# A hybrid attention block on one Trainium2 core: PSUM shared out as two banks for the projections' products and three for scores, instead of three and two

## The chip, the cores and the metric

The kernel runs on one core of a Trainium2 chip. The metric is device time in microseconds (us). TensorE multiplies matrices and writes its sums to PSUM, a memory of eight banks of 2 KB in each of 128 partitions. VectorE (DVE), ScalarE (ACT) and GpSimd (POOL) do elementwise work; SyncE (SP) issues the DMAs between the core's SBUF and the chip's memory. Each engine has its own instruction queue and runs it in order. An instruction whose operand or whose output buffer is not ready stops everything behind it on its engine, and on no other.

## The reference, cut to what matters

One block of a model for 2048 tokens of width 1024, in float32:

```python
# ada: six vectors (scale, shift, gate for the mixer and the FFN) from the condition c
h = rmsnorm(x, g_mix) * (1 + scale) + shift
p = h @ w_in                        # 1024 -> 2 x 256 (gating), 3 x 384 (stick), 3 x 384 (dilated)
a = gelu(u) * (causal 128x128 mixing of rmsnorm(gelu(v)) + b_sp)        # spatial gating, 4 groups

# stick-breaking attention, 6 heads of 64, every key before the query:
z = q @ k.T / 8
weight = sigmoid(z) * prod over the keys between of sigmoid(-z)
o_b = weight @ v

# dilated window attention, 6 heads, 129 keys at distances 0, d, ... 128 d with d = 1, 4, 16:
z = q @ k_gathered.T / 8;  pr = softmax(z);  o_c = pr @ v_gathered     # q and k rotated (rope)
o_c *= softmax over the three d of the log of each softmax's denominator

x = x + gate * (concat(a, o_b, o_c) @ w_out)
x = x + gate2 * convffn(rmsnorm(x))       # up to 2 x 2816, causal convolution of 3 taps, gate, down
out = rmsnorm(x) * g_final
```

## The kernel before, in words

**Products.** Each float32 operand is split into a high and a low part, and a product is three matmuls (high x high, low x high, high x low; L100 to L102). An input projection of a 128-wide block of features for 512 tokens thus takes 8 x 3 = 24 matmuls of 512 columns into one PSUM bank, the tile `gm`; one for values takes 48 matmuls of 256 columns into the tile `gmv`, which has the tag `gm` too. When the last of them is done, ScalarE or VectorE copies the bank to SBUF: as tile `stage`, for queries and keys (then stored to the chip's memory in `bq`, `bk` or, rotated, `cq`, `ck`), or as `vst`, for values. That copy is called the eviction below.

**Stages.** The tokens are worked in two halves of 1024, c = 0 and c = 1. Up to 97 us lie the conditioning vectors, the norm of the first tokens and the first projections. Then come projections, the six stick heads of the first half, the gating of the first half, and the projections of the second half, one stick head of the first half (at about 520 to 580 us) and the six dilated heads of all tokens (460 to 776 us) beside them. From 776 us the second half's stick heads run beside the output projection. The conv-FFN takes from about 1320 us to the end.

**A stick head** (`stick`) loads keys (`khat`, L83) and queries (`q`). For each block of 128 queries and up to 512 keys it has two score matmuls into a bank `z` (L534, L537, and L536 where the causal border lies in the block), two sigmoids on ScalarE (L539 to SBUF as `beta`, L540 back into the bank), a scan along the keys on VectorE (L545, `excl`), which is the last reader of the bank and frees it, a multiply on GpSimd (L78), transposes back on TensorE into a bank `tr` (L554), two copies of that as high and low part (`wh`, `wl`), and the product with the values into the bank `av` (L565). **A dilated head** (`dilated`) has the same shape: scores into a bank `zc` of tag `z` (L620, L621), mask and maximum on VectorE (L623, last reader of the bank), the exponential on ScalarE (L632, `ec`), transposes `trc` (L635), product `avc` (L658). After each 512 queries `fold` (L487) adds the two halves of `av` or `avc` into the one buffer `ys`, which is stored (`yT`, `yc`) before the next sum may be written.

**What sets the order.** Buffers come from pools with a count for each tag (the table `BUFS`): a tile waits until the last reader of the tile that had its slot before is done. In PSUM up to the end of the first half's attentions and all dilated heads there is the pool `ps`: eight banks, as `gm` 3, `z` 2, `tr` 2, `av` 1. At the token `rel` of the string `ORDER` it is given back and the pool `ps2` taken, with `gm` 2 and `z` 3 (L1102). The order in which each engine's queue is filled is chosen when the program is built, by a scheduler that takes ready instructions by their place in the program and by durations that it assumes; the counts of the pools thus change the queues of all engines. On TensorE matmuls of a projection and of an attention stand mixed, so that the one fills the time in which the other waits. The first four query and key products of all (L910, L925) are filled in parts as the conditioning vectors come, in banks named one by one.

Of the kernel before, what the change touches and what calls it, by code (L numbers as in the profile page):

```python
# [5 lines left out]
F32 = mybir.dt.float32  # L6
# [6 lines left out]
PSUM = bass.MemoryType.PSUM  # L13
DRAM = bass.MemoryType.DRAM

P = 128
# [5 lines left out]
TG = 512  # L22
# [21 lines left out]
class Kernel:  # L44
# [810 lines left out]
    def run(self):  # L855
        tc, nc, i = self.tc, self.nc, self.i
        self.constants()
        self.ps = _Bufs(self.pool("ps", space=PSUM), BUFS)
        self.p1 = _Bufs(self.pool("p1"), BUFS)
        self.pa = _Bufs(self.pool("pa", side="right"), BUFS)  # L860
        dr = self.dr
# [27 lines left out]
        def h_cols(c, tg, xs, ks=range(KB)):  # L889

            if hT[c][0][tg] is None:
                hT[c][0][tg], hT[c][1][tg] = self.act_tiles(self.p1, "h", tg)
            self.norm_cols(self.p1, self.ps, "tr", xs, self.cols["a1"], self.cols["s1"], hT[c][0][tg], hT[c][1][tg], ks,
                           ("lnt0", "hlo0") if c == 0 and tg == 0 else ("lnt", "hlo"))
# [5 lines left out]
        def qk_cols(p):  # L900
# [6 lines left out]
        near = (self.p1, "whi"), (self.p1, "wlo")  # L907
        places = ((near, near), (near, ((self.pa, "khat"), (self.pa, "khat"))),
                  (((self.pa, "vhat"), (self.pa, "khat")), ((self.pa, "vhat"), (self.pa, "wl"))))
        banks = [self.ps.tile([P, TG], F32, name="gm", tag=tag) for tag in ("gm", "gm", "gm", "z")]  # L910
        vbanks = [self.ps.tile([P, 2, 256], F32, name="gmv", tag=tag) for tag in ("z", "av")]
        for q in range(4):
            self.ada_first(q)
# [110 lines left out]
        def work(units, what, n, c):  # L1024

            b_qk, c_qk, v, a = units
            if what == "bqk":
                return b_qk(n)
            if what == "cqk":
                return c_qk(n, cs)  # L1030
            if what == "v":
                return v(n)
            if what == "a":
                return a()
            if what == "wout":
                return self.out_weights(ada[2])
            if what == "op":
                return self.out_proj(0)
            return self.out_proj(1, EARLY)

        def finish(names=None):

            while aside and (names is None or any(x[0] in names for x in aside)):
                for _ in aside.pop(0)[1]:
                    pass

        for c, order in enumerate(ORDER):
            u = units(c, hT[c])
            for token in order.split():
                name = token.lstrip("~")  # L1050
# [18 lines left out]
                elif what in ("bqk", "cqk", "v", "a", "wout", "op", "oa"):  # L1069
                    for _ in work(u, what, n, c):  # L1070
                        pass
                    if behind:
                        behind.__exit__(None, None, None)
                        behind = None
                elif what == "vh":
                    finish()
                    if xs is None:
                        xs = h_rows(1, 0)
                    xs2 = []

                    def middle():
                        h_cols(1, 0, xs)
                        xs2.append(h_rows(1, 1))
                    for _ in u[2](n, {1: middle, 3: lambda: h_cols(1, 1, xs2[0])}):
                        pass
                elif what == "hr":
                    xs = h_rows(1, 0)
                elif what == "rope":
                    cs = self.rope_tables(c)
                elif what == "ada":  # L1090
                    with tc.issue_after(self.stored.ins):
                        ada[n] = self.ada_rest(n)
                elif what == "dil":
                    finish([f"cqk{n // 2}{c}", f"v{(6 + n) // 4}{c}"])
                    self.dilated(n)
                elif what == "scales":
                    self.dilated_scales()
                elif what == "rel":
                    finish()
                    self.p1.release()  # L1100
                    self.ps.release()
                    self.ps = _Bufs(self.pool("ps2", space=PSUM), {**BUFS, "gm": 2, "z": 3})  # L1102
                    self.po = _Bufs(self.pool("po"), BUFS)
                elif what == "free":
                    finish()
                    self.pa.release()
                    self.pw = _Bufs(self.pool("pw", side="right"), BUFS)
                    self.pn = _Bufs(self.pool("pn", side="right"), BUFS)
# [43 lines left out]

ENGINES = {"whi0": "a", "wlo0": "v", "lnt0": "a", "hlo0": "v", "lnt": "va", "lnx00": "avv", "lnx01": "aav", "lnx10": "v", "lnx11": "v", "lnx": "va", "hlo": "v", "whi": "a", "wlo": "v", "qkhi": "avv", "qklo": "v", "cqk": "a", "rot1": "v", "rot2": "v", "rot3": "v", "rothi": "aav", "rotlo": "v", "sgu1": "v", "sgu2": "v", "sguhi": "a", "sgulo": "v", "ya": "aaav", "fold": "a", "beta": "p", "whi_s": "a", "whi_d": "avv", "wom": "v", "wohi": "aav", "wolo": "v", "ysc": "v", "yhi": "av", "ylo": "v", "wuhi": "v", "wulo": "pvv", "wdm": "p", "wdhi": "av", "wdlo": "ppv", "upc": "av", "gv": "pppv", "ghi": "ap", "glo": "ppv", "vhi": "av", "vlo": "v", "uc": "v"}

BUFS = {"gm": 3, "z": 2, "tr": 2, "av": 1, "wraw": 2, "whi": 3, "wlo": 3, "s8": 3, "cs": 2, "tmp2": 2, "khat": 3, "vhat": 2, "q": 2, "beta": 4, "excl": 3, "wh": 2, "wl": 2, "fold": 1, "ys": 1, "stat": 2, "mx": 2, "x4": 2, "yraw": 2, "ysc": 4, "yh": 2, "yl": 2, "xo": 3, "wuraw": 4, "wul": 3, "wuh": 3, "wdraw": 2, "fx": 2, "up": 3, "dn": 5, "wdh": 2, "wdl": 2, "upc": 3, "cv": 3, "gh": 4, "gl": 4, "fs": 4, "fry": 2, "frr": 2}

WOUT = 6
EARLY = (0, 1, 5, 6, 7)
# [39 lines left out]
```

## Time and profile before

| | |
|---|---|
| median of 3 runs | 2775.93 us (2775.42 to 2779.58) |
| the profiled execution | 2772.08 us |
| its span, first to last instruction | 2770.4 us |
| mean granted TensorE clock | 0.981 |
| TensorE busy | 2626.6 us, 95%, 13430 matmuls |
| VectorE busy | 2109.4 us, 76% |
| ScalarE busy | 1025.6 us, 37% |
| GpSimd busy | 857.5 us, 31% |
| chain that ended last, by engine | PE 65%, DVE 14%, DMA 10%, ACT 6%, issue 3% |

The program on the chip takes the span and about 1.7 us around it. TensorE's matmuls overlap their neighbours in the records (one of 512 columns is recorded as 0.39 us long and follows the one before by less), so a busy share near 100% does not say that nothing is lost; gaps and the clock tell more. The shares are means over stages: the FFN, from 1320 us on, is more than half of the span and has no tile of this pool.

### The profile page before, as it was taken

What the parts mean: (1) busy time and instruction counts of PE and PEld (TensorE: products, weight loads), DVE (VectorE), ACT (ScalarE), POOL (GpSimd) and SP (SyncE); (2) the same over time, 40 slices, a digit from 0 to 9 for tenths busy, and PEclk for the clock granted to TensorE, in tenths of its full rate; (3) what the DMA queues carried; (4) which work ended last, traced back from release to release, by engine and by line L of the source; (5) the groups of instructions that cost most, each with busy time, mean ns of one, the idle gap of its engine ahead of it and who ended that gap; (6) DMA issues with size and microseconds to landing.
All of it is one profiled execution on the core that took longest, in us unless ns stands there. A gap on an engine that the chain in (4) does not pass through costs nothing.

```text
span 2770.4 us, 36801 instructions
## 1 busy us (share of the span) xinstructions
PE 2626.6 (95%) x13430; PEld 2201.3 (79%) x13430; DVE 2109.4 (76%) x3227; ACT 1025.6 (37%) x1918; POOL 857.5 (31%) x878
## 2 busy tenths in 40 slices
PE   6989999899878999999999999999999999999998
PEld 5878998889857777877788888888877888888886
DVE  5487877666689988756877778777888778777877
ACT  5355554444556666534121212111462111121114
POOL 0032101110045444303334443433433433433423
PEclk9999999999999999999999999999999999999999
DMA  7645586789563333286111111111233111111111
GB/s 238 195 131 171 186 266 190 204 211 233 135 186 101 109 111 86 61 275 219 46 46 46 54 51 49 48 52 46 77 103 107 49 47 54 46 46 46 46 38 61
DMA packets 305296, 309.37 MB, mean 112 GB/s; under 512 B 65516, under 2 KB 245596, under 8 KB 305116
## 3 DMA queue, kind: packets, MB, share of 16 engines
q1 hardware_dynamic: 305116, 307.02, 37.6%
q8 instruction: 107, 1.75, 0.3%
q14 instruction: 73, 0.60, 0.1%
HBM read 232.36 MB, written 68.30 MB: 109 GB/s over the span
## 4 chain that ended last, share of the span: by engine, by line
PE 65%; DVE 14%; DMA 10%; ACT 6%; issue 3%; SPq 1%; POOL 0%; DVEq 0%; ACTq 0%; POOLq 0%
PE up L94 11%; PE up L93 11%; PE up L92 11%; PE dn L94 5%; PE dn L92 5%; PE dn L93 5%; DVE excl L545 3%; DMA wraw<-in_w_in_dram 2%; PE gmv L342 2%; DMA wada<-in_w_ada_dram 2%; PE av L565 2%; DVE wl L78 1%; PE gm L100 1%; PE tr L554 1%; PE gm L101 1%
## 5 line engine op out<-in xcount | busy, mean ns | idle before, releaser
L92 PE MATMUL up<-gh,wuh 128*128 128x512 f32 x1408 | 553.4, 393 | 2.1 <-ACT gh L260 2.1
L94 PE MATMUL up<-gh,wul 128*128 128x512 f32 x1408 | 554.9, 394 | 0.0
L93 PE MATMUL up<-gl,wuh 128*128 128x512 f32 x1408 | 554.5, 394 | 0.0
L78 POOL TENSOR_TENSOR beta<-beta,excl 128x127 f32<-128x127 f32 (+2 forms) x240 | 267.5, 1116 | 869.6 <-DVE excl L545 758.5
L829 DVE TENSOR_TENSOR acc<-dn,acc 128x512 f32<-128x512 f32 x688 | 440.7, 680 | 104.2 <-PE dn L94 102.0
L787 DVE SCALAR_TENSOR_TENSOR cv<-upc,cw,cv 128x512 f32<-128x512 f32 x352 | 334.8, 952 | 104.9 <-ACT cv L785 101.6
L92 PEld LDWEIGHTS up<-gh,wuh 128*128 128x128 f32 x1408 | 265.0, 188 | 62.1 <-ACT gh L260 2.3
L93 PEld LDWEIGHTS up<-gl,wuh 128*128 128x128 f32 x1408 | 265.1, 188 | 61.3 <-issue 0.2
L94 PEld LDWEIGHTS up<-gh,wul 128*128 128x128 f32 x1408 | 265.1, 188 | 60.0 <-issue 0.2
L92 PE MATMUL dn<-wdh,gh 128*128 128x512 f32 x688 | 270.9, 395 | 10.6 <-DVE acc L829 9.4
L93 PE MATMUL dn<-wdl,gh 128*128 128x512 f32 x688 | 270.9, 394 | 0.0
L94 PE MATMUL dn<-wdh,gl 128*128 128x512 f32 x688 | 256.1, 395 | 0.0
L785 ACT ACTIVATE cv<-up,cb 128x512 f32<-128x512 f32 x176 | 136.4, 775 | 290.9 <-DVE upc L72 290.9
L545 DVE TENSOR_TENSOR_SCAN excl<-z,excl,beta 128x512 f32<-128x512 f32 x144 | 183.3, 1275 | 14.9 <-ACT z L540 13.2
L70 ACT ACTIVATE upc<-up 128x512 f32<-128x512 f32 x88 | 52.4, 596 | 373.8 <-PE up L94 373.8
L70 ACT ACTIVATE wh<-tr 128x128 fp32r<-128x128 f32 (+2 forms) x240 | 127.7, 535 | 168.4 <-PE tr L554 164.8
L72 DVE CAST wuh<-wuraw 128x512 fp32r<-128x512 f32 x176 | 129.0, 771 | 62.0 <-PE up L93 59.7
L342 PE MATMUL gmv<-whi,hh 128*128 128x256 f32 x576 | 167.0, 291 | 0.7 <-DVE vst L78 0.7
L342 PE MATMUL gmv<-wlo,hh 128*128 128x256 f32 x576 | 166.6, 290 | 0.3 <-DVE wlo L78 0.3
L342 PE MATMUL gmv<-whi,hl 128*128 128x256 f32 x576 | 166.7, 291 | 0.0
L78 DVE TENSOR_TENSOR wl<-tr,wh 128x128 fp32r<-128x128 f32 (+2 forms) x240 | 141.9, 594 | 31.6 <-ACT wh L70 31.6
L92 PEld LDWEIGHTS dn<-wdh,gh 128*128 128x128 f32 x688 | 129.8, 189 | 42.6 <-DVE acc L829 11.6
(238 smaller groups left out, 5594.8 us busy)
## 6 DMA issues: line engine op xcount, KB each, us to landing
wuraw<-in_w_up_dram SPq DMA_DIRECT2D x176, 256.0 KB, 3.2
wdraw<-in_w_down_dram SPq DMA_DIRECT2D x44, 512.0 KB, 3.5
wada<-in_w_ada_dram SPq DMA_DIRECT2D x32, 512.0 KB, 6.2
wraw<-in_w_in_dram SPq DMA_DIRECT2D x112, 128.0 KB, 4.3
vd<-vst SPq DMA_DIRECT2D x12, 1024.0 KB, 6.0
q<-bq SPq DMA_DIRECT2D x48, 256.0 KB, 4.2
q<-cq SPq DMA_DIRECT2D x48, 256.0 KB, 5.5
x<-xo SPq DMA_DIRECT2D x24, 512.0 KB, 5.2
```

Of the source, the lines that this page charges most:

```text
L70: self.nc.scalar.activation(out, in_, AF.Copy)
L72: self.nc.vector.tensor_copy(out, in_)
L78: (self.nc.vector if eng == "v" else self.nc.gpsimd).tensor_tensor(out=out, in0=a, in1=b, op=op)
L92: self.nc.tensor.matmul(ps, ah, bh, start=(k == 0), stop=False)
L93: self.nc.tensor.matmul(ps, ah, bl, start=False, stop=False)
L94: self.nc.tensor.matmul(ps, al, bh, start=False, stop=(k == n - 1))
L342: self.nc.tensor.matmul(ps[:, e, :], a[:, o:o + P], b, start=(n == 0), stop=(n == 3 * KB - 1))
L545: nc.vector.tensor_tensor_scan(x[:, x0:x0 + n][:, ::-1], z[:, :n][:, ::-1], b[:, :n][:, ::-1], before, op0=ALU.mult, op1=ALU.bypass)
L565: last = nc.tensor.matmul(av[:, q0:256], vhat[kc // 2][:, (kc % 2) * 4 + e, :], w[:, e, q0:256], start=(kc == top and m == 0), stop=(kc == ...
L785: nc.scalar.activation(t, ps, AF.Identity, bias=self.cb[:, blk:blk + 1], scale=self.cw[2][:, blk:blk + 1])
L787: nc.vector.scalar_tensor_tensor(out=t, in0=u[:, tap:tap + TG], scalar=self.cw[tap][:, blk:blk + 1], in1=t, op0=ALU.mult, op1=ALU.add)
L829: nc.vector.tensor_tensor(out=acc[t][:, ns], in0=ps, in1=acc[t][:, ns], op=ALU.add)
```

## The change

The pool `ps` gets two banks for `gm` and three for `z`; `tr` and `av` stay. The pool `ps2` takes the table as it is, which now has the counts that were written out for it, so that nothing changes there. The third of the first four products goes into a bank of tag `z` instead of `gm`.

```diff
-        banks = [self.ps.tile([P, TG], F32, name="gm", tag=tag) for tag in ("gm", "gm", "gm", "z")]
+        banks = [self.ps.tile([P, TG], F32, name="gm", tag=tag) for tag in ("gm", "gm", "z", "z")]
         vbanks = [self.ps.tile([P, 2, 256], F32, name="gmv", tag=tag) for tag in ("z", "av")]
...
-                    self.ps = _Bufs(self.pool("ps2", space=PSUM), {**BUFS, "gm": 2, "z": 3})
+                    self.ps = _Bufs(self.pool("ps2", space=PSUM), BUFS)
...
-BUFS = {"gm": 3, "z": 2, "tr": 2, "av": 1, "wraw": 2, "whi": 3, "wlo": 3, "s8": 3, ...
+BUFS = {"gm": 2, "z": 3, "tr": 2, "av": 1, "wraw": 2, "whi": 3, "wlo": 3, "s8": 3, ...
```

No instruction is added or taken away, but the scheduler fills the queues in another order. On every engine the orders are alike up to the first stick head, and again nearly alike from the second half's first stick head (`z_8433`) on. Three places follow; the number behind a name counts the tiles of the program, and is the same in both.

The first is on TensorE, at the first stick head (about 113 to 121 us). Before, its first two scores, `z_1127` and `z_1141`, stand behind all 24 matmuls of the projection tile `gm_2217` and 6 of the next, `gm_2243`:

```order
L100 MATMUL gm_2243<-hh_716,whi_2192 128x512
L101 MATMUL gm_2243<-hl_724,whi_2192 128x512
L102 MATMUL gm_2243<-hh_716,wlo_2193 128x512
L534 MATMUL z_1127<-khat_1117,q_1121 128x128
L536 MATMUL z_1127<-after_678,ident_r_676 128x128
L537 MATMUL z_1127<-khat_1117,q_1121 128x128
L534 MATMUL z_1141<-khat_1117,q_1121 128x256
L536 MATMUL z_1141<-after_678,ident_r_676 128x128
```

Now three scores of this head stand behind the first 8 of the 24 matmuls of `gm_2217`:

```order
L100 MATMUL gm_2217<-hh_233,whi_2192 128x512
L101 MATMUL gm_2217<-hl_241,whi_2192 128x512
L534 MATMUL z_1127<-khat_1117,q_1121 128x128
L536 MATMUL z_1127<-after_678,ident_r_676 128x128
L537 MATMUL z_1127<-khat_1117,q_1121 128x128
L534 MATMUL z_1141<-khat_1117,q_1121 128x256
L536 MATMUL z_1141<-after_678,ident_r_676 128x128
L537 MATMUL z_1141<-khat_1117,q_1121 128x256
L534 MATMUL z_1162<-khat_1117,q_1121 128x384
L536 MATMUL z_1162<-after_678,ident_r_676 128x128
L537 MATMUL z_1162<-khat_1117,q_1121 128x384
L102 MATMUL gm_2217<-hh_233,wlo_2193 128x512
```

They have moved ahead by 22 matmuls of 512 columns. On SyncE the load of their keys (`khat_1117`) stands ahead of the two stores of `bq10` from `stage_996`, and behind them before; ahead of that both queues have the same DMAs there.

The second is ScalarE and TensorE where the first half's rotation tables are made (about 150 to 160 us). `gm_2284` and `gm_2310` are two projection tiles whose evictions ScalarE does one after the other into `stage_2283`. Before, ScalarE has them here, behind the transposed weights `tr_1272`; the cosine and the sine stand 9 and 8 rows ahead of the first of them, ahead of the sigmoids of `z_1305`:

```order
L70 ACTIVATE wh_1247<-tr_1257 128x4x128
L539 ACTIVATE beta_1335<-z_1332 128x512
L540 ACTIVATE z_1332<-z_1332 128x512
L70 ACTIVATE wh_1247<-tr_1272 128x4x128
L70 ACTIVATE stage_2283<-gm_2284 128x512
L70 ACTIVATE stage_2283<-gm_2310 128x512
L539 ACTIVATE beta_1350<-z_1347 128x512
L540 ACTIVATE z_1347<-z_1347 128x512
L70 ACTIVATE rot_2275<-rot_2275 128x1024
```

Now the sigmoids of `z_1305` and `z_1332` stand ahead of the cosine, and those of `z_1347` and `z_1401`, with the copy of `tr_1299`, between the sine and the evictions:

```order
L381 ACT_TABLE_LOAD
L381 ACTIVATE cos_1378<-cos_1378,halfpi_1089 128x1024
L382 ACTIVATE sin_1377<-sin_1377,sign_1084 128x1024
L70 ACTIVATE wh_1247<-tr_1272 128x4x128
L539 ACT_TABLE_LOAD
L539 ACTIVATE beta_1350<-z_1347 128x512
L540 ACTIVATE z_1347<-z_1347 128x512
L70 ACTIVATE wh_1287<-tr_1299 128x3x128
L539 ACTIVATE beta_1405<-z_1401 128x128
L540 ACTIVATE z_1401<-z_1401 128x128
L70 ACTIVATE stage_2283<-gm_2284 128x512
L70 ACTIVATE stage_2283<-gm_2310 128x512
```

On TensorE the tile `gm_2375`, which now takes the bank of `gm_2284`, has its 24 matmuls right behind the last of `gm_2310` before:

```order
L101 MATMUL gm_2310<-hl_730,whi_2204 128x512
L102 MATMUL gm_2310<-hh_722,wlo_2205 128x512
L100 MATMUL gm_2375<-hh_231,whi_2350 128x512
L101 MATMUL gm_2375<-hl_239,whi_2350 128x512
L102 MATMUL gm_2375<-hh_231,wlo_2351 128x512
```

Now 42 rows of the stick heads stand between the two, and then `gm_2375`:

```order
L565 MATMUL av_1211<-wh_1247,vhat_1119 128x256
L565 MATMUL av_1211<-wl_1248,vhat_1119 128x256
L565 MATMUL av_1211<-wh_1247,vhat_1119 128x256
L565 MATMUL av_1211<-wl_1248,vhat_1119 128x256 x2
L554 MATMUL tr_1315<-ident_60,beta_1309 128x128 x4
L100 MATMUL gm_2375<-hh_231,whi_2350 128x512
L101 MATMUL gm_2375<-hl_239,whi_2350 128x512
L102 MATMUL gm_2375<-hh_231,wlo_2351 128x512
```

The evictions have moved behind the sigmoids of two more score tiles and one more copy, and the start of `gm_2375` behind work of the stick heads alone.

The third is ScalarE near the end of the dilated heads (about 700 to 720 us). Before, the split of a weight tile, `whi_8207`, and a gelu (`u_7827`) stand ahead of the exponentials of the last head, `ec_7046` and `ec_7069`:

```order
L70 ACTIVATE whi_7889<-wraw_7895 128x512
L70 ACTIVATE fold_6962<-avc_6928 64x512
L70 ACTIVATE whc_7012<-trc_7005 128x512
L70 ACTIVATE whi_8207<-wraw_8209 128x512
L425 ACT_TABLE_LOAD
L425 ACTIVATE u_7827<-u_7827 128x1024
L632 ACT_TABLE_LOAD
L632 ACTIVATE ec_7046,stat_7040<-ec_7046,mx_7041 128x128 x2
L632 ACTIVATE ec_7069,stat_7040<-ec_7069,mx_7041 128x128 x2
```

Now the exponentials of this head begin ahead of the splits of `whi_7889`, and the gelu and `whi_8207` stand 6 and 8 rows behind the second of these:

```order
L632 ACTIVATE ec_7046,stat_7040<-ec_7046,mx_7041 128x128 x2
L632 ACTIVATE ec_7069,stat_7040<-ec_7069,mx_7041 128x128 x2
L70 ACTIVATE fold_7023<-avc_6989 64x512
L632 ACTIVATE ec_7099,stat_7040<-ec_7099,mx_7041 128x128 x2
L632 ACTIVATE ec_7122,stat_7040<-ec_7122,mx_7041 128x128 x2
L70 ACTIVATE fold_7091<-avc_7063 64x512
L632 ACTIVATE ec_7152,stat_7040<-ec_7152,mx_7041 128x128 x2
L70 ACTIVATE whc_7112<-trc_7107 128x2x128
L632 ACTIVATE ec_7175,stat_7040<-ec_7175,mx_7041 128x128 x2
L70 ACTIVATE whi_7889<-wraw_7891 128x512
L70 ACTIVATE whi_7889<-wraw_7895 128x512
```

`ec_7046` and `ec_7069` have moved from behind `whi_8207` to 18 and 17 rows ahead of it. TensorE's queue has the last head's `avc` tiles closer together than before: the first matmuls of the last four (`avc_7063`, `avc_7116`, `avc_7169`, `avc_7222`) stand 46, 50 and 41 rows apart, and 54, 48 and 73 before.

## Rows read from the trace of the kernel before

**Rows 1.** Windows: stretch, length, busy us of each engine, PEclk, DMA share, GB/s.
```profile
460.00:520.00 60.00, 53.19 (x356) 49.31 (x355) 44.24 (x86) 18.64 (x49) 0.00 (x0) 0.91 0.97 261
...
580.00:700.00 120.00, 115.29 (x845) 107.52 (x844) 75.68 (x249) 53.60 (x157) 0.00 (x0) 1.00 0.91 231
700.00:776.00 76.00, 67.56 (x469) 63.19 (x468) 45.58 (x129) 35.95 (x76) 0.00 (x0) 0.93 0.56 131
```

**Rows 2.** Waits of TensorE, 60 to 170 us: us in total, times, longest.
```profile
PE z L534 <- DVE excl L545: 5.0, 3, 3.6
```

**Rows 3.** Waits of TensorE, 170 to 520 us.
```profile
PE z L534 <- DVE excl L545: 5.5, 7, 3.1
```

**Rows 4.** Waits of TensorE, 520 to 600 us.
```profile
PE z L534 <- DVE excl L545: 4.5, 1, 4.5
```

**Rows 5.** Waits of TensorE, 700 to 770 us.
```profile
PE trc L635 <- ACT ec L632: 8.4, 2, 7.5
```

**Rows 6.** Waits of TensorE, 45 to 770 us, the whole stretch of the change.
```profile
PE trc L635 <- ACT ec L632: 14.1, 8, 7.5
...
PE zc L620 <- DMA khat<-ck: 3.5, 1, 3.5
PE zc L620 <- DVE stat L623: 3.0, 3, 1.3
```

**Rows 7.** Windows right after four of these waits.
```profile
157.00:164.00 7.00, 5.95 (x15) 4.75 (x16) 7.00 (x7) 4.59 (x9) 4.34 (x3) 0.51 0.47 108
243.00:246.00 3.00, 3.00 (x14) 3.00 (x15) 3.00 (x4) 0.87 (x2) 2.12 (x2) 0.52 0.00 0
536.00:539.00 3.00, 3.00 (x8) 2.32 (x8) 2.08 (x5) 1.36 (x5) 1.83 (x3) 0.50 0.92 263
714.00:724.00 10.00, 5.06 (x25) 5.07 (x26) 4.24 (x15) 7.61 (x17) 0.00 (x0) 0.51 0.85 187
```

**Rows 8.** Timeline of TensorE: start, duration, line, operation, [idle before it].
```profile
118.70 0.39 PE L102 MATMUL gm<-hh,wlo 128*128 128x512 f32 x1
118.93 0.39 PE L100 MATMUL gm<-hh,whi 128*128 128x512 f32 x1
...
120.33 0.33 PE L534 MATMUL z<-khat,q 128*128 128x128 f32 x1 [0.55 <-DMA khat<-bk]
```

**Rows 9.** Timeline of TensorE at 158 us.
```profile
158.05 0.80 PE L534 MATMUL z<-khat,q 128*128 128x512 f32 x1 [3.62 <-DVE excl L545]
```

**Rows 10.** Timeline of TensorE in the dilated attention.
```profile
707.03 0.28 PE L342 MATMUL gmv<-wlo,hh 128*128 128x256 f32 x1
707.15 0.28 PE L342 MATMUL gmv<-whi,hl 128*128 128x256 f32 x1
```

**Rows 11.** Timeline of SyncE's DMA queue.
```profile
112.27 1.24 SPq L83 DMA_DIRECT2D bq<-stage  x2
...
114.38 0.75 SPq L83 DMA_DIRECT2D khat<-bk  x1
```

**Rows 12.** Timeline of ScalarE at 150 to 160 us.
```profile
154.30 1.28 ACT L539 ACT_TABLE_LOAD   x1
...
158.55 1.10 ACT L70 ACTIVATE stage<-gm 128x512 f32<-128x512 f32 x2
```

**Rows 13.** Timeline of TensorE, the last matmul of `gmv_5267`.
```profile
488.65 0.28 PE L342 MATMUL gmv<-whi,hl 128*128 128x256 f32 x1
```

**Rows 14.** Timeline of ScalarE, the evictions of `gmv_5267` and the next.
```profile
504.73 0.64 ACT L70 ACTIVATE vst<-gmv 128x256 fp32r<-128x256 f32 x2
```

**Rows 15.** Timeline of ScalarE at the end of the dilated heads.
```profile
714.08 0.63 ACT L70 ACTIVATE whi<-wraw 128x512 fp32r<-128x512 f32 x1 [8.13 <-DMA wraw<-in_w_in_dram]
...
718.39 0.40 ACT L632 ACTIVATE ec<-ec,mx 128x128 f32<-128x128 f32 x1
```

**Rows 16.** The chain that ended last, 600 to 730 us: start, us, what.
```profile
637.05 7.37 DMA yc<-ys
```

**Rows 17.** DMA issues: KB each, median us from issue to landing.
```profile
yc<-ys SPq DMA_DIRECT2D x24, 128.0 KB, 5.5
```

More of the change, by code (lines that the diff above doesn't have):

```diff
@@ L1153 @@
 ENGINES = {"whi0": "a", "wlo0": "v", "lnt0": "a", "hlo0": "v", "lnt": "va", "lnx00": "avv", "lnx01": "aav", "lnx10": "v", "lnx11": "v", "lnx": "va", "hlo": "v", "whi": "a", "wlo": "v", "qkhi": "avv", "qklo": "v", "cqk": "a", "rot1": "v", "rot2": "v", "rot3": "v", "rothi": "aav", "rotlo": "v", "sgu1": "v", "sgu2": "v", "sguhi": "a", "sgulo": "v", "ya": "aaav", "fold": "a", "beta": "p", "whi_s": "a", "whi_d": "avv", "wom": "v", "wohi": "aav", "wolo": "v", "ysc": "v", "yhi": "av", "ylo": "v", "wuhi": "v", "wulo": "pvv", "wdm": "p", "wdhi": "av", "wdlo": "ppv", "upc": "av", "gv": "pppv", "ghi": "ap", "glo": "ppv", "vhi": "av", "vlo": "v", "uc": "v"}
-BUFS = {"gm": 3, "z": 2, "tr": 2, "av": 1, "wraw": 2, "whi": 3, "wlo": 3, "s8": 3, "cs": 2, "tmp2": 2, "khat": 3, "vhat": 2, "q": 2, "beta": 4, "excl": 3, "wh": 2, "wl": 2, "fold": 1, "ys": 1, "stat": 2, "mx": 2, "x4": 2, "yraw": 2, "ysc": 4, "yh": 2, "yl": 2, "xo": 3, "wuraw": 4, "wul": 3, "wuh": 3, "wdraw": 2, "fx": 2, "up": 3, "dn": 5, "wdh": 2, "wdl": 2, "upc": 3, "cv": 3, "gh": 4, "gl": 4, "fs": 4, "fry": 2, "frr": 2}
+BUFS = {"gm": 2, "z": 3, "tr": 2, "av": 1, "wraw": 2, "whi": 3, "wlo": 3, "s8": 3, "cs": 2, "tmp2": 2, "khat": 3, "vhat": 2, "q": 2, "beta": 4, "excl": 3, "wh": 2, "wl": 2, "fold": 1, "ys": 1, "stat": 2, "mx": 2, "x4": 2, "yraw": 2, "ysc": 4, "yh": 2, "yl": 2, "xo": 3, "wuraw": 4, "wul": 3, "wuh": 3, "wdraw": 2, "fx": 2, "up": 3, "dn": 5, "wdh": 2, "wdl": 2, "upc": 3, "cv": 3, "gh": 4, "gl": 4, "fs": 4, "fry": 2, "frr": 2}
 WOUT = 6
```

## The prediction, made before the changed kernel ran

> **What bounds the kernel now.** TensorE is busy for 95% of the span, so the first question is where its 5% are, and whether the change reaches them. It can reach only the tiles of the first PSUM pool, up to 776 us. I went first through the windows by stage: in the stretch of the first dilated heads, 460 to 520 us, TensorE is busy for 53.19 of 60 us at a mean clock of 0.91, and in the last one, 700 to 776 us, for 67.56 of 76 us at 0.93; between 580 and 700 us it is nearly full, with DMA at 0.91 of its capacity [rows 1]. Then the waits of TensorE say which buffer or value it stood for. The scores of the stick heads waited for a z bank, freed by the scan on VectorE: 5.0 us up to 170 us, 5.5 us from there to 520 us and 4.5 us once at 535 us [rows 2 to 4]. The dilated heads waited 14.1 us for exponentials, 3.0 us for a bank freed by the maximum, and 3.5 us for keys on their way [rows 6]. Next to nothing was lost to a projection that stood for its gm bank. So the third gm bank is spare where the second z bank is short, and that is the argument for a gain.
>
> The windows behind the long waits show a second price: after a wait of some 3 us TensorE's clock is granted at its lower level, 1.2 instead of 2.4 GHz: 0.51, 0.52, 0.50 and 0.51 in four stretches of 7, 3, 3 and 10 us [rows 7]. The time lost there is length times one minus the clock: 3.4, 1.4, 1.5 and 4.9 us. Beside the Trainium skill's page "TensorE: Matmul & The Clock Gate", section "A second HAM failure mode: psum-queue depth-cycling", these rows agree: it says that a kernel that cycles through PSUM banks with brief idle times between its groups lost throughput by the clock's changes though its matmuls at full clock were as fast as another's. That rule speaks for a third z bank and, with the same force, against taking one from gm.
>
> **What goes.** With three banks a score tile waits for the scan of the third tile before it, not the second. The order puts the scores 5 to 18 us of TensorE's work earlier, and the transposes that need them no earlier, so both the wait for the bank and the wait for the result shrink. I count as gone:
> - the z waits after 170 us, 5.5 + 4.5 = 10.0 us [rows 3, 4], and the half-speed stretches behind two of them, 1.4 + 1.5 = 2.9 us [rows 7];
> - the waits at 700 to 770 us, 8.4 us [rows 5], and 4.9 us of clock [rows 7]. Here ScalarE's queue decides: it stood 8.13 us at the split of a weight tile whose load had not landed, and the exponentials behind it came only at 718.39 [rows 15]. In the new order they stand ahead of that split. The split's own readers, the matmuls of the last query and key projection, stand behind the last `avc` in TensorE's queue and cover it there; if the load lands later still, that projection is what is late next;
> - half of the other waits for exponentials, (14.1 - 8.4) / 2 = 2.8 us, and the 3.0 us for the bank of zc [rows 6].
> Sum 32.0 us. The lower bound for this is nothing (each wait comes back at the next tile), the upper 36 us, with 2.8 us more for the exponentials and 1.4 us of the first z waits.
>
> **What comes.** Five places, all read from the order and priced by rows of before.
>
> First, the keys of the first stick head. Its scores stand 22 matmuls of 512 columns earlier, and one such takes 118.93 - 118.70 = 0.23 us [rows 8]: 5.0 us. TensorE already waited 0.55 us for these keys [rows 8]. Their load is passed ahead of two stores alone, which took 1.24 us of SyncE's queue [rows 11]; so TensorE arrives 5.0 us earlier and the keys 1.24 us: 3.8 us more of waiting. All of the projections, queued behind on the same engine, stand with it. Bounds 0 (the head starts its long chain earlier, and TensorE gets it back) and 5.0 us.
>
> Second, `gm_2375`. Before, TensorE stood 3.62 us at a score at 158 us [rows 9], while ScalarE made the cosine and sine with two table loads, the second at 154.30, and evicted two projection tiles at 158.55 [rows 12]. Now the evictions stand behind the sigmoids of two more score tiles and a copy, and the projection that needs the bank stands behind the score work. The stall of 3.62 us therefore moves from the score to the projection and grows. By the nearest row, 1.10 us for two tiles of 512 columns [rows 12], five more ScalarE instructions of up to that width are 5 x 0.55 = 2.75 us: I take 2.7. Bounds -3.6 (the stall goes, since the scores now run ahead) and +7, where the half-speed stretch of 3.4 us doubles too.
>
> The Trainium skill's page "Perfetto Trace Analysis", section "Optimizing Tensor Performance", says under "Matmuls" that groups of matmuls should rotate through PSUM banks so that the eviction of one overlaps the next group's matmuls. By it two banks are enough wherever an eviction is done within one group, 24 x 0.23 = 5.5 us, an estimate from [rows 8]. The trace agrees only in part: at 158.55 ScalarE evicted tiles that had long been complete. By that rule this step and the next but one would cost nothing, which is the third rival.
>
> Third, the first dilated keys. Before, TensorE waited 3.5 us for them [rows 6], and behind it 7 us ran at half speed. The score now stands 11 matmuls earlier: 11 x 0.23 = 2.5 us more, if the load lands when it did. Bounds -3.5 and 5 us.
>
> Fourth, the value projection of the second half. `gmv_5267` was complete at 488.93 us (488.65 + 0.28) and evicted at 504.73 [rows 13, 14], 15.8 us later, because ScalarE and the buffers of the stores kept it. Before, `gmv_5375` had a third bank. Now 59 rows of TensorE stand between the end of `gmv_5267` and the start of `gmv_5375`, 59 x 0.12 = 7.0 us by the pace of these matmuls (707.15 - 707.03 [rows 10]), and `gmv_5267` ends 39 rows later than it did, 4.7 us: 15.8 - 7.0 - 4.7 = 4.1 us of stall. Bounds 0 and 8.8 us, with a half-speed stretch like the last of [rows 7], 4.9 us, behind it.
>
> Fifth, the one buffer `ys`. Near the end the `avc` tiles of a head stand 41 to 50 rows apart instead of 48 to 73, 4.9 to 6.0 us of matmuls. A tile can be folded only when the sum before it has landed: 5.5 us in the median from issue [rows 17], 7.37 us in the worst step of the chain [rows 16], and the sum and its issue, about 1.2 us, around that. That is some 7 us for each tile, against a pace of 5.5: about 2 us for each of the four last tiles, 8 us in all. Bounds 0 (the stage doesn't come to that pace) and 15.
>
> Nothing is priced on GpSimd, VectorE and the c = 1 stage: their instructions are the same, and their order from 776 us on is nearly so; the FFN hides nothing of this, it just starts earlier.
>
> Sum: -32.0 + 3.8 + 2.7 + 2.5 + 4.1 + 8 = -10.9 us, against the profiled execution's 2772.08: 2761.2. The median of the runs shown is 3.85 above that execution, so 2765.0 is the forecast.
>
> **The rivals.**
> - *Two gm banks are too few* (slower). One mechanism: a projection group stands for its bank until ScalarE, deep in score work, evicts, and all scores behind it in TensorE's queue stand with it; then the lower clock follows. For it: tiles evicted long after completion at 158.55 and 504.73. Against it: no wait for gm with three banks, and most evictions follow soon. Price: the upper ends at the second and fourth place and for ys, 7 + 8.8 + 4.9 + 15, with 3.8 and 2.5: 42.0 less 32.0, or 10 us slower: 2785.9. It decides once these five places together take more than 37 us, or where as many of the gains don't come.
> - *The waits move and the time stays.* Between 460 and 700 us DMA works at 0.91 to 0.97 of its capacity [rows 1], and the chain that ended last goes through stores of `ys` and loads of weights there. If they set the pace, TensorE waits in other places for the same total: the 13 us at 700 us come back as 15 at ys, the rest nets out. Against it: outside 460 to 580 us TensorE is nearly full, and its matmuls are no fewer. Time: 2775.9, give or take 5.
> - *Two banks cost nothing.* Place two and four at zero, ys at zero: -32.0 + 6.3 = -25.7, or 2750.2. For it: no gm wait before. Against it: the same rows as for the first rival.
>
> **How the numbers follow.** The forecast, a gain between 6 and 20 us, has 0.42; the third rival 0.13; no net change 0.18; the slower one 0.27. About 0.2%, 5.5 us, is what a measurement here can tell from no change. So faster is 0.55, same 0.18, slower 0.27. The range takes in the third rival's time with 3 us to spare and the first one's with 2: 2747 to 2788; the likeliest case's own is 2756 to 2770.
>
> **What would show it.** In the changed kernel's profile: waits of z for the scan after 170 us under 3 us in all, and no half-speed stretch at 243 and 536 us; at the end of the dilated heads no wait of 7 us for exponentials. Against me, step by step: a wait of some 4 us for the first keys, a gm wait behind a `stage` or `vst` eviction at about 160 and 505 us, the longest of all if the first rival is right, and `ys` waits on its store above the 9 us or so of before. The prediction is wrong in its direction if gm waits and their half-speed stretches exceed 18 us, and wrong in its mechanism if the z waits stay.

## The result, and the profile after

| | before | after |
|---|---|---|
| median | 2775.42 us (5 runs, 2770.91 to 2779.58) | 2811.63 us (5 runs, 2805.14 to 2818.85) |
| ratio | 1 | 1.0135, 95% interval 1.0119 to 1.0151 |
| span of the profiled execution | 2770.4 us | 2806.5 us |
| mean granted TensorE clock | 0.981 | 0.977 |

The change is slower by 1.35%, some 37 us, above the range of the prediction and on the other side of its forecast. From the second half's stick heads on the two traces run nearly alike, 36 to 42 us apart; the loss is made ahead of that.

The waits of TensorE in the changed kernel, 45 to 812 us, which holds about the same work as 45 to 770 us before (4430 and 4415 matmuls); us in total, times, longest:

```profile
PE zc L620 <- DMA q<-cq: 14.8, 10, 3.3
PE zc L620 <- issue: 6.7, 1, 6.7
PE av L565 <- DVE wl L78: 6.0, 4, 2.1
...
PE av L565 <- DVE ys L487: 4.3, 2, 2.4
PE z L534 <- DVE excl L545: 4.0, 4, 2.2
PE gm L102 <- DVE wlo L78: 3.5, 1, 3.5
PE zc L620 <- DMA khat<-ck: 3.5, 1, 3.5
PE gmv L327 <- DVE hl L78: 3.3, 3, 1.9
...
PE gmv L342 <- DVE vst L78: 2.6, 1, 2.6
PE ya_ps L454 <- DVE u L449: 2.3, 1, 2.3
...
PE gm L100 <- DVE vst L78: 1.6, 1, 1.6
PE mix_ps L443 <- ACT vs L70: 1.6, 1, 1.6
...
PE trc L635 <- ACT ec L632: 1.0, 1, 1.0
...
PE zc L620 <- DVE stat L623: 0.5, 1, 0.5
```

Read it against [rows 2 to 6]. What was to go went: z from 15.0 (5.0 + 5.5 + 4.5) to 4.0 us, trc from 14.1 to 1.0, the bank of zc from 3.0 to 0.5, together 26.6 us. But the rows at the top are new: 14.8 + 6.7 us for the dilated heads' queries, none before, and 6.0 + 4.3 us for the stick heads' products, 1.0 us before. All waits of this stretch add up to 50 us before and 73 us after. The rest of the loss is about what the clock took: the span times one minus the mean clock is 2770.4 x 0.019 = 52.6 us before and 2806.5 x 0.023 = 64.6 us after. Some 24 us of waits and some 12 us of clock make the 36 us between the spans. In the stretch of the change alone the clock takes more: by its windows 725 x 0.03 = 22 us before and 767 x 0.05 = 38 us after (length, busy us of PE, PEld, DVE, ACT, POOL, clock, DMA share, GB/s; before's first).

```profile
45.00:770.00 725.00, 676.34 (x4415) 611.36 (x4416) 502.74 (x970) 351.06 (x732) 89.24 (x73) 0.97 0.68 189
```

```profile
45.00:812.00 767.00, 695.12 (x4430) 628.92 (x4431) 513.71 (x971) 347.36 (x731) 83.43 (x73) 0.95 0.64 179
```

Only two of the rows shown, gmv and gm behind `vst`, 4.2 us together, are projections that stood for a bank. So in the list of waits the loss looks only in small part like a lack of gm banks. It looks like work that nothing covers: attention above all, 31.8 us in the four rows just named. The windows show how full TensorE was, before's first and then after's:

```profile
300.00:460.00 160.00, 157.71 (x1091) 145.46 (x1090) 126.24 (x205) 82.23 (x145) 17.42 (x15) 1.00 0.70 222
```

```profile
300.00:460.00 160.00, 144.02 (x1023) 135.24 (x1024) 119.13 (x202) 75.93 (x139) 17.35 (x15) 0.97 0.62 193
312.00:487.00 175.00, 161.68 (x1089) 149.36 (x1088) 125.94 (x203) 77.59 (x138) 16.54 (x13) 0.97 0.66 204
493.00:500.00 7.00, 6.41 (x25) 5.46 (x26) 6.97 (x13) 2.59 (x4) 0.00 (x0) 0.76 0.95 297
604.00:612.00 8.00, 7.17 (x27) 5.95 (x28) 7.35 (x19) 0.56 (x3) 0.00 (x0) 0.79 0.84 210
747.00:757.00 10.00, 9.72 (x63) 9.75 (x64) 4.47 (x22) 3.40 (x14) 0.00 (x0) 0.71 0.47 125
```

The stretch from 300 to 460 us was the fullest before, 157.71 of 160 us with 1091 matmuls; now it has 144.02 us with 1023. The changed kernel is already some 12 us behind at its start, so the same work lies at about 312 to 487 us: it takes 15 us longer. What stands bare there isn't attention. TensorE waits 12.9 us from 312 to 487 us (1.9 us before, 300 to 460): 4.7 us for the gating (`ya_ps`, `mix_ps`), 4.2 us for a projection's bank, 2.0 us for a weight's low part and 2.0 us for the norm. The three short windows stand right behind waits for keys or queries and show the half-speed stretches, 0.71 to 0.79 on the mean of the window.

The first loss lies ahead of the first stick head, where "The change" says that the orders are alike. On TensorE they aren't. Before, 19 matmuls of the projection tile `gm_911` stand between those of two value tiles and run while the next `hl` is made. Now both gm banks hold those value tiles, `gm_911` stands behind them, and TensorE waits (before's row, then after's with the window behind it):

```profile
84.30 0.39 PE L315 MATMUL gm<-hh,whi 128*128 128x512 f32 x1
```

```profile
87.45 0.58 PE L327 MATMUL gmv<-whi,hl 128*128 128x256 f32 x1 [1.94 <-DVE hl L78]
```

```profile
87.00:91.00 4.00, 3.55 (x18) 3.55 (x19) 0.40 (x1) 0.00 (x0) 0.00 (x0) 0.57 0.75 265
```

That is 1.94 us of waiting and 4.00 x 0.43 = 1.7 us of clock, and it is the plainest place where the third bank held work that covered a wait.

The places of the prediction, in the timeline of the changed kernel's TensorE (start, duration, line, operation, idle before it and what ended that):

```profile
120.85 0.30 PE L534 MATMUL z<-khat,q 128*128 128x128 f32 x1 [1.35 <-DMA bq<-stage]
...
155.20 0.33 PE L565 MATMUL av<-wl,vhat 128*128 128x128 f32 x1 [2.12 <-DVE wl L78]
...
161.77 0.42 PE L565 MATMUL av<-wh,vhat 128*128 128x256 f32 x2 [2.43 <-DVE ys L487]
...
167.77 0.39 PE L565 MATMUL av<-wl,vhat 128*128 128x256 f32 x1 [1.89 <-DVE wl L78]
...
168.94 0.62 PE L100 MATMUL gm<-hh,whi 128*128 128x512 f32 x1
...
493.59 0.44 PE L620 MATMUL zc<-khat,q 128*128 128x128 f32 x1 [3.48 <-DMA khat<-ck]
...
747.28 0.45 PE L620 MATMUL zc<-khat,q 128*128 128x128 f32 x1 [6.66 <-issue]
```

The first score waited 1.35 us, not 4, and the profile puts that down to a store of `bq` instead of the keys; near 162 us TensorE stood for `ys` in a stick head, not for a projection's bank (more on this below); the first dilated keys cost 3.48 us, as before (3.5, [rows 6]); and the last row is the new wait of 6.66 us in the stretch where the wait of 7.5 us for exponentials had been [rows 5]. What stood behind the waits from 155 to 168 us is the bank all the same. `gm_2284` and `gm_2310` hold both gm banks until ScalarE evicts them:

```profile
167.41 1.09 ACT L70 ACTIVATE stage<-gm 128x512 f32<-128x512 f32 x2
```

```profile
155.00:173.00 18.00, 13.49 (x56) 11.44 (x57) 18.00 (x23) 14.38 (x24) 10.90 (x7) 0.72 0.43 104
```

The next projection, `gm_2375`, starts at 168.94; before it started at 141.19. From the end of `gm_2310` at 151.1 us on TensorE has no projection's matmul to run, stands 6.4 us in the three waits shown and works at a clock of 0.72 in that window (0.28 x 18.00 = 5.0 us). Before, 3.62 us of waiting [rows 9] and 3.4 us of clock [rows 7] were lost there. No row of it names the bank, since the scheduler has put the projection behind the attention's work.

What the last row waited for stands in the same kernel's DMA queue on SyncE:

```profile
733.26 6.62 SPq L83 DMA_DIRECT2D vhat<-vd  x2
739.98 1.24 SPq L83 DMA_DIRECT2D q<-cq  x2
```

The load of the queries was issued at 739.98, behind two loads of values that held the queue for 6.62 us. It is the kind of wait that had been read for the weights in [rows 15], an engine's queue held at its head by something else, on another queue.

### The profile page after: what moved, and what is told of

It reads as the page before. It is cut to its first block, busy times and chain, and to the rows that moved or that the text cites. A ratio compares the mean times of both kernels' runs of the same rounds, so it can differ in the third digit from the quotient of the medians.

```text
span 2806.5 us, 36810 instructions
## 1 busy us (share of the span) xinstructions
PE 2637.3 (94%) x13430; PEld 2212.8 (79%) x13430; DVE 2120.1 (76%) x3227; ACT 1021.7 (36%) x1916; POOL 847.1 (30%) x878
## 4 chain that ended last, share of the span: by engine, by line
PE 66%; DVE 13%; DMA 12%; ACT 4%; issue 3%; SPq 2%; POOL 0%; DVEq 0%; ACTq 0%
PE up L92 11%; PE up L93 11%; PE up L94 11%; PE dn L94 5%; PE dn L92 5%; PE dn L93 5%; PE gmv L342 4%; DVE excl L545 3%; DMA wada<-in_w_ada_dram 2%; PE av L565 2%; SPq L83 2%; DMA q<-cq 1%; DMA wraw<-in_w_in_dram 1%; DVE wl L78 1%; PE gm L100 1%
## 5 line engine op out<-in xcount | busy, mean ns | idle before, releaser
L78 POOL TENSOR_TENSOR beta<-beta,excl 128x127 f32<-128x127 f32 (+2 forms) x240 | 259.5, 1084 | 910.3 <-DVE excl L545 709.9
L545 DVE TENSOR_TENSOR_SCAN excl<-z,excl,beta 128x512 f32<-128x512 f32 x144 | 183.5, 1275 | 14.8 <-ACT z L540 13.2
L78 DVE TENSOR_TENSOR wl<-tr,wh 128x128 fp32r<-128x128 f32 (+2 forms) x240 | 141.9, 593 | 27.8 <-ACT wh L70 27.8
```

The costliest lines, as they stand in the source:

```text
L78: (self.nc.vector if eng == "v" else self.nc.gpsimd).tensor_tensor(out=out, in0=a, in1=b, op=op)
L545: nc.vector.tensor_tensor_scan(x[:, x0:x0 + n][:, ::-1], z[:, :n][:, ::-1], b[:, :n][:, ::-1], before, op0=ALU.mult, op1=ALU.bypass)
```

## The experiments

The runs e1, e2, e5 to e11, e15, e17 and e18 give the banks their roles by stage. A small class replaces the pool: it has five banks `b0` to `b4`, gm takes the one of the first two or three whose last use lies longest back, z of the last two or three, and the numbers can be changed at a token of `ORDER`. With three and two TensorE's order is that of before but for one move of eight matmuls near the start.

```diff
+    def mode(self, gm, z):
+        self.roles = {"gm": [f"b{k}" for k in range(gm)], "z": [f"b{4 - k}" for k in range(z)]}
...
+                if (c, token) in MODES:
+                    self.ps.mode(*MODES[c, token])
```

Ratios are to runs of before on the same chip, with their 95% intervals; us are ratio times 2773.

| run | banks (gm, z) | ratio | us |
|---|---|---|---|
| e1 | 2, 3 in the first half; 3, 2 then | 1.0120 [1.0098, 1.0143] | +33 |
| e2 | 3, 2; 2, 3 from the second half's program on | 1.0022 [1.0007, 1.0038] | +6 |
| e3 | 2, 2, one bank idle | 1.0153 [1.0130, 1.0176] | +42 |
| e4 | 3, 3, and 1 for tr | 1.0582 [1.0560, 1.0605] | +161 |
| e9 | 2, 2 up to cqk1 | 1.0053 [1.0036, 1.0070] | +15 |
| e5 | 2, 2 for cqk1, cqk2 | 1.0043 [1.0029, 1.0057] | +12 |
| e6 | 2, 2 for cqk0, gating, v2 | 1.0014 [0.9998, 1.0030] | +4 |
| e7 | 2, 2 for bqk2, vh1 | 1.0019 [1.0002, 1.0036] | +5 |
| e18 | 2, 2 from the second half to dil3 | 1.0015 [0.9998, 1.0032] | +4 |
| e17 | 2, 2 from dil3 on | 0.9999 [0.9984, 1.0014] | 0 |
| e10 | 2, 3 from dil3 on | 1.0038 [1.0023, 1.0052] | +11 |

**Which bank, and which half.** e1 and e2 split the change at the second half's program, e3 leaves out the third score bank, e4 has both. Theory 1 of the expectations is that the missing gm bank costs, theory 2 that the third z bank does, theory 3 that any other order does.

```diff
 e1  _Swap(pool, 2, 3);  MODES = {(1, "ada2"): (3, 2)}
 e2  _Swap(pool, 3, 2);  MODES = {(1, "ada2"): (2, 3)}
 e3  BUFS  "gm": 2, "z": 2;  first banks ("gm", "gm", "tr", "z")
 e4  BUFS  "gm": 3, "z": 3, "tr": 1
```

> Two gm and three z banks up to the end of the first half's program, three and two from there on (the dilated heads). Theory 1 (two product banks: the projections come later, and the first half's chains lose their cover): the trace of the changed kernel is 26 us behind when the first dilated score runs, so about 2801 us. Theory 2 (three score banks: the dilated heads' scores run ahead to the wait for their queries' loads): no more than 2785 us. Theory 3 (any other order of the queues costs some): between, with waits that neither kernel has.

> Three gm and two z banks in the first half, two and three from the second half's program on. Theory 1: the lag that the changed kernel gains behind its first dilated score is 12 us, and some of it is the bank of the last value projections: 2775 to 2787 us, and waits for loaded queries in the dilated heads are few. Theory 2: 2787 us or more, with 10 us or more of waits of zc for q. If both stages add up, e1 and e2 together lose 36 us.

> Two gm and two z banks, the eighth bank unused (the third of the first four products goes to a tr bank). Theory 1: as slow as the changed kernel or slower, 2811 to 2830 us, since the third z bank gave something. Theory 2: the loss of the dilated stage goes, 2775 to 2800 us, and no waits of zc for q.

> Three gm and three z banks, one bank for the transposes instead of two. Theory 1: gains of the third z bank without the loss, 2755 to 2775 us, unless the one transpose bank costs (then waits of tr for its copies show it). Theory 2: slower than before by 10 us or more with waits of zc for q.

e1 and e2 lose 33 and 6 us, and the change 37: the two parts add up, and most of it is the first half. e3 decides between the first two theories: without any third score bank the kernel is as slow as the changed one (1.0153 against 1.0135, with intervals that overlap). The gm bank costs all of it, and the z bank gives nothing for it that these runs can tell. The waits of e3, 45 to 815 us:

```profile
PE avc L658 <- DVE ys L487: 6.4, 2, 4.9
...
PE z L534 <- DVE excl L545: 4.3, 5, 1.7
...
PE gm L100 <- ACT stage L70: 3.6, 2, 3.1
...
PE gm L100 <- DVE vst L78: 3.5, 1, 3.5
```

The z waits are down to 4.3 us with two z banks, too: for that the third one wasn't needed. All waits of this stretch add up to 74 us in e3 and to 73 in the changed kernel, but in other rows. The dilated heads' queries, the top rows of the changed kernel with 21.5 us, take 2.5 us in e3, and `ys` and others take their place. So the longest rows of a list of waits needn't be what the loss hangs on. In e3 projections stand 7.1 us for their bank (the two gm rows). e4 was to show the gain without the loss and showed another limit: one transpose bank costs 161 us, and its kernel waits for queries and transposes (45 to 940 us):

```profile
PE zc L620 <- DMA q<-cq: 26.9, 10, 4.6
PE tr L554 <- DVE wl L78: 15.9, 9, 6.2
```

**Which stage.** e9, e5, e6, e7 take a gm bank away in one stage of the first half each, with z at two.

```diff
 e9  _Swap(pool, 2, 2);  MODES = {(0, "cqk1"): (3, 2)};  first banks ("gm", "gm", "tr", "z")
 e5  _Swap(pool, 3, 2);  MODES = {(0, "cqk1"): (2, 2), (0, "cqk0"): (3, 2)}
 e6  _Swap(pool, 3, 2);  MODES = {(0, "cqk0"): (2, 2), (0, "~bqk2"): (3, 2)}
 e7  _Swap(pool, 3, 2);  MODES = {(0, "~bqk2"): (2, 2), (1, "ada2"): (3, 2)}
```

> Two gm and two z banks (as e3) up to the first stick heads' projections, three and two from cqk1 on: what e3 loses ahead of the place where e5 begins. e3 lost 38.5 us, e5 to e7 12, 4 and 5, and e2 4.6 of it with three z banks: 4 to 11 us slower than before, 2778 to 2785 us, if the parts add up; under 3 us if they don't.

> Three gm and two z banks as before, but two gm (z stays at two) for the projections that run beside the first stick heads, cqk1 and cqk2; the order differs from before only from the tile gm_2375 on. Theory 1a (the loss is spread: every stage in which TensorE has a third projection to fill with loses some): 5 to 12 us slower, 2779 to 2786 us. Theory 1b (it is one place): either all 30 us here or less than 4.

> Two gm (two z) for the next projections alone, cqk0, the gating's and v2. Theory 1a: 5 to 12 us slower, 2779 to 2786 us, with waits of mix_ps and ya_ps as in the changed kernel. Theory 1b: all 30 us here or less than 4.

> Two gm (two z) for the last projections of the first half's program, bqk2 and the values vh1. Theory 1a: 5 to 12 us slower, 2779 to 2786 us. Theory 1b: all 30 us here or less than 4. If the three stages add up, e5 to e7 together lose about 30 us; if the loss is of the kind that any other order costs, they don't add up.

15, 12, 4 and 5 us: spread, as theory 1a says, with the more of it early. e6 alone can't be told from no change, and e6 and e7 lose no more than another order alone can (e13 and e14, below). Nor is a stage's loss all made in the stage: the order stays another one for a while behind it. In e5's trace the 1338 matmuls from 114 us on take 223 us and 221 before, and the next 670 or so, behind the place where the third bank is back, take 104 us and 96 before.

**Is any other order dearer?** e10, with the change in the last stage alone, was forecast to gain and lost 11 us. e12 moves the evictions of the rotated projections from ScalarE to VectorE and changes no bank; e11 does the same and takes the gm bank of e5 away. Both speak for a plainer theory: that the order of before is tuned, and any other costs some 10 us.

```diff
 e10       _Swap(pool, 3, 2);  MODES = {(1, "dil3"): (2, 3)}
 e11, e12  ENGINES  -"cqk": "a"  +"cqk": "v"
 e13       ORDER    -st3 st0     +st0 st3
 e14       ORDER    -dil3 dil5   +dil5 dil3
```

> Two gm and three z banks from the token dil3 on alone, that is from about 563 us. In the trace of before the third gm bank is really in use there three times (the next but one product starts before the tile is evicted), for 0.9, 1.2 and 0.8 us, while up to 520 us it is 17 times and for up to 18 us. Theory 1, in the form that the loss is where the third bank is in use: no loss here, and what the third z bank gives shows: 2762 to 2774 us. Rival (any other order costs): 2777 to 2785 us.

> e5 with the rotated projections' evictions on VectorE instead of ScalarE, to be compared with e12. If the banks of e5 are held too long by ScalarE's queue (33 us for gm_2284 in before), the loss of 12 us against its own base shrinks to 6 us or less. If the hold doesn't matter, it stays at about 12 us.

> The base for e11: the kernel before with the rotated projections' evictions on VectorE. Within 10 us of before on either side (VectorE is busy for 109 of 140 us there, so rather slower).

e12 took 1.0032 [1.0019, 1.0044], 9 us more than before, and e11 1.0038 [1.0024, 1.0052]: on that base the gm bank of e5 costs 0.0006 instead of 0.0043. But this doesn't show that ScalarE's hold was the reason: in e12's trace the next but one projection still starts up to 20 us ahead of an eviction. So e13 and e14 change the order with no bank, buffer or engine:

> The kernel before with its second and third stick heads (st3, st0) in the other order: no buffer, bank or instruction changes, only the order. If any other order costs: 5 to 12 us slower. If the banks' use is what costs: within 4 us of before.

> The kernel before with two dilated heads (dil3, dil5) in the other order, which changes the queues from about 563 us on, where e10 lost 10 us. If any other order costs: 5 to 12 us slower. If two gm and three z banks are what cost in e10: within 4 us of before.

e13 took 1.0016 [1.0004, 1.0027], e14 0.9980 [0.9968, 0.9992]: 4 us slower and 6 us faster. Another order alone moves this kernel by some 5 us on either side; it doesn't cost 10 everywhere. e14, with the two heads exchanged, is the one kernel here that is faster than both, 0.2% below before.

**Is the bank's use what counts?** In before one can ask of each projection tile whether the next but one started ahead of the tile's eviction; then three banks were in use. The tiles' names come from the order, the times from the trace: `gm_2284` was evicted from 158.55 to about 159.2 [rows 12], and `gm_2375`, the next but one, had started here, in before's timeline of TensorE:

```profile
141.19 0.39 PE L100 MATMUL gm<-hh,whi 128*128 128x512 f32 x1
```

That is 18.0 us of use. From 112 to 790 us it is 19 tiles and 87 us in all (e10's text counts one tile too many): 19 us in the stage of e5, 53 in that of e18, 3 in that of e17 (three tiles). e17 and e18 take the gm bank away there and leave z at two.

```diff
 e17  _Swap(pool, 3, 2);  MODES = {(1, "dil3"): (2, 2)}
 e18  _Swap(pool, 3, 2);  MODES = {(1, "ada2"): (2, 2), (1, "dil3"): (3, 2)}
```

> Two gm and two z banks from dil3 on, as e10 without its third z bank. If a gm bank costs where it is in use: within 4 us of before, since there the third one is used for 2.9 us in all, and the 10 us of e10 are the third z bank's (scores that run into the waits for q and ys). If two gm banks cost everywhere: 2778 us or more.

> Two gm and two z banks from the second half's program to dil3, where the trace of before has the third gm bank in use for 53 of 87 us. If a gm bank costs where it is in use: the largest loss of the stages, 8 to 20 us. If use doesn't matter: 4 us or less, or as much as e17.

e17 is the same as before to 0.0015: where the third bank is hardly used, it can go. e18 lost 4 us, not the 8 to 20 forecast, and can't be told from no change. So use tells where a bank is spare, and not how much it is worth where it is not.

In this stage the missing bank does show as a wait for the bank. The tile `gm_5181` stands for the eviction of `gm_5114`, in e2 and then in e18:

```profile
475.41 0.79 PE L100 MATMUL gm<-hh,whi 128*128 128x512 f32 x1 [6.43 <-ACT stage L70]
```

```profile
475.19 0.79 PE L100 MATMUL gm<-hh,whi 128*128 128x512 f32 x1 [3.16 <-ACT stage L70]
```

With the waits behind `vst` (1.7 and 1.6 us) that is 8.1 us in e2 and 4.8 in e18, whose whole losses were 6 and 4 us. The stages with two and two, e9, e5, e6, e7, e18 and e17, add up to 0.0143; e3, which is all of them at once, lost 0.0153.

e10 less e17 is the third z bank in the last stage: 11 us dearer. The waits of both, 563 to 780 us, e10's first, and then a window of both, in the same order:

```profile
PE zc L620 <- DMA q<-cq: 6.3, 6, 2.4
PE avc L658 <- DVE ys L487: 3.5, 1, 3.5
PE zc L620 <- issue: 2.9, 1, 2.9
```

```profile
PE zc L620 <- DMA q<-cq: 7.2, 4, 2.3
PE trc L635 <- ACT ec L632: 3.7, 2, 2.3
```

```profile
640.00:700.00 60.00, 54.55 (x450) 53.62 (x449) 40.69 (x135) 28.09 (x87) 0.00 (x0) 0.97 0.92 238
```

```profile
640.00:700.00 60.00, 57.38 (x487) 56.88 (x488) 40.63 (x131) 31.10 (x87) 0.00 (x0) 1.00 0.82 213
```

With three z banks there are two more kinds of wait, for `ys` and for a late issue, and in the window TensorE is busy for 54.55 us with 450 matmuls at a clock of 0.97, against 57.38 us with 487 at 1.00. But this doesn't show where the 11 us come from. Over the whole stage, 563 to 780 us, the waits add up to 14.5 us in e10 and 14.3 in e17, and TensorE is busy for 202.5 and 202.4 us. These two executions lie 6.6 us apart, and 3.4 us of it was there at the first matmul at which the queues differ. What the windows show besides is some 3 us more of half speed in e10. The cause of the rest is open.

**The next limit.** If scores that run ahead only meet the next buffer, more of that should help. e8 is e2 with a third buffer for the dilated heads' queries; e15 is e10 with that and a second `ys`, and e16 is before with both. They were lent from the three slots of `excl`.

```diff
-        q = self.pa.tile([P, 2, 512], F32, name="q")
+        q = self.pa.tile([P, 2, 512], F32, name="q", tag=tag)         # "q", "q", "excl" in turn
...
-                ys = self.pa.tile([64, 512], F32, name="ys", tag="ys")
+                ys = self.pa.tile([64, 512], F32, name="ys", tag=...)  # "ys", "excl" in turn (e15, e16)
```

> As e2 (two gm and three z banks from the second half's program on), and a third buffer for the dilated heads' queries, lent by the tag of excl. If the third z bank's gain in the dilated heads was eaten by waits for query loads, these go and 2762 to 2770 us come out, below both kernels. If z banks don't matter there: 2774 to 2782 us, as e2.

> e10 with a third buffer for the dilated heads' queries and a second ys, both lent by the tag of excl. If the late stage has a chain of next limits (z bank, then q, then ys: e10 waits for q, e8 for ys), the waits go here and 2755 to 2770 us come out. If DMA (0.9 to 1.0 of its capacity from 585 to 640 us) or the order sets the pace: 2774 to 2785 us.

> The base for e15: the kernel before with the same two extra buffers and its own banks (gm three, z two). If z is the limit that hides q and ys: no gain, 2770 to 2778 us. If q or ys already cost something in before: 2760 to 2768 us.

All three are misses: 1.0036 [1.0022, 1.0051], 1.0106 [1.0087, 1.0126] and 1.0128 [1.0113, 1.0142]. In e8, at 585 to 800 us, the waits did move on as the theory says, from the queries to `ys`:

```profile
PE avc L659 <- DVE ys L487: 8.6, 3, 3.9
PE zc L621 <- DMA q<-cq: 3.3, 1, 3.3
```

but nothing was won. e16 waits for one load of queries longer than any kernel here:

```profile
779.83 0.45 PE L621 MATMUL zc<-khat,q 128*128 128x128 f32 x1 [13.79 <-DMA q<-cq]
```

```profile
740.00:780.00 40.00, 19.02 (x98) 16.70 (x98) 15.80 (x47) 10.51 (x31) 0.00 (x0) 0.59 0.62 148
```

From 740 to 780 us TensorE is busy for 19 of 40 us at a clock of 0.59: the projections had been used up earlier, and the last heads ran bare. The lent slots tie queries and sums to the scans' buffers, so that these runs don't say what buffers of their own would do.

## Why the prediction was wrong

The step that failed is in the first part: "Next to nothing was lost to a projection that stood for its gm bank. So the third gm bank is spare where the second z bank is short". The first sentence is right; the second doesn't follow. Next to no wait was seen since there were three banks, and they were in use, for 87 us. When one is taken, the order is laid anew, and the loss comes only in part as a wait for the bank (4.2 us in the changed kernel, 4.8 to 8.1 in e18, e3 and e2). For the rest projections come later, and what they had covered stands bare: attention, gating, norm, and at 85 us the wait for `hl`, with the lower clock behind many of the gaps. e3 puts the whole loss on the gm bank; e17 is the counter-example in which the bank was spare indeed. That the lost cover is the way from the bank to the time is read from the traces, and no run shows it by itself.

Point by point:

- *What goes.* The waits went as forecast, 26.6 us against 24.2. The clock's 7.8 us did not come back: in all 12 us more were lost to it, and in the stretch of the change some 16. And "each wait comes back at the next tile", the lower bound, was nearest: 21.5 us of new waits for queries alone.
- *First keys, 3.8 us.* 1.35 us, 0.8 more than before, and 2.23 us behind it for a scan: the size is right by chance, the place half right.
- *`gm_2375`, 2.7 us.* In the changed kernel the tile was late by 27.8 us, as read here from the order, but the stall showed as waits for `ys` and `wl` in the stick heads, 6.4 us, and not at the bank. e5, whose order first differs at the same tile, lost 12 us, the most of it behind its stage.
- *First dilated keys, 2.5 us.* Nothing: 3.48 against 3.51 us. Their loads had moved as well.
- *`gmv_5375`, 4.1 us.* No such wait in the changed kernel, where `gmv_5267` stood 0.8 us for `stage`. The kind of wait was right: in e2 and e18 `gm_5181` stood 6.43 and 3.16 us for its bank near there.
- *`ys` at the end, 8 us.* Not for `ys`: TensorE waited for queries there, which the prediction hadn't priced at all.
- *The rivals.* The first, "two gm banks are too few", was right in its name, and had a chance of 0.27. Its price of 10 us was a quarter of the loss: it counted places at which a projection would stand for its bank, and such waits were 4.2 us in all. The clock, named beside the Trainium skill's page "TensorE: Matmul & The Clock Gate", section "A second HAM failure mode: psum-queue depth-cycling", was said to speak against taking a gm bank with the same force as for z; that held, and the sum had used it for z alone.
- *The rule of eviction.* By the page "Perfetto Trace Analysis" of the Trainium skill, section "Optimizing Tensor Performance", under "Matmuls", groups rotate so that an eviction overlaps the next group. Here two banks do that only where the third was not in use: e17 yes, e3 no.

Open: why a stage's loss is not in the proportion of the bank's use there (19 us of use cost 12 us in e5, 53 us cost 4 in e18), and why moving the evictions to VectorE made e5's loss vanish in e11. Before's exact order with a bank less was not tried, so what the bank costs and what the order laid for fewer banks costs are not told apart, beyond that an exchange of heads alone moved the time by some 5 us either way.

## What to carry to other kernels

A buffer that nobody waits for is not spare: count how often its last slot was filled, and take it only where that is nearly never. Where matmuls of one kind cover the chains of another, a change of buffers can be paid where the cover goes missing, as waits of the covered work and as a lower clock, more than as waits for the buffer. And when a wait for one buffer goes, look up what the same instruction needs next, here the loads of its queries and their place in the DMA queue. A list of waits says what stood, not what it would be worth to take a row away: e3 has the same sum of waits in other rows.

## What the runs showed that was not expected

One transpose bank instead of two, with the third z bank beside it, cost 161 us (e4), four times the gm bank. And the clock is a second price beside the waits: with 24 us more waits the changed kernel lost 12 us more to half speed.
